# A two-layer hybrid decoder: last down projection and final norm turned from feature-major to token-major

## The chip, the core and the metric

The kernel runs on one core of a Trainium2 chip. The metric is the device time of one execution in microseconds. The core has a matrix engine (TensorE; PE in the rows), a vector engine (VectorE, DVE), an activation engine (ScalarE, ACT), a general engine (GpSimd, POOL), and SyncE (SP), which here only issues DMAs. Each engine works through its own instructions in order; semaphores order the engines among each other. Sixteen DMA engines move data between the device memory and the on-chip memory of 128 partitions. TensorE adds up in PSUM, eight banks of 128 x 512 floats.

## The reference

Input x has 512 tokens and 1024 features, in float32. There are two layers; each has a mixer (three branches, gated and summed) and a feed-forward part, and behind both stands one norm. What the change touches is the end of the second layer:

```python
    x = x + jnp.einsum('bsd,de->bse', merged, w_out[layer])
    h2 = rmsnorm(x, ffn_norm[layer])
    gu = jnp.einsum('bsd,df->bsf', h2, w_gate_up[layer])
    x = x + jnp.einsum('bsf,fd->bsd', jax.nn.silu(gu[..., :D_FF]) * gu[..., D_FF:], w_down[layer])
return rmsnorm(x, final_norm)
```

rmsnorm divides each token's 1024 features by the root of their mean square (plus 1e-6) and multiplies feature by feature with a weight vector. D_FF is 2816, that is 22 tiles of 128.

## The kernel before

Nearly all matmuls are products of split operands. A float32 value is held as a high part (a cast to fp32r) and a low part (the rest), and each product is three matmuls: high by high, high by low, low by high. The weights are split on the chip: `wload` loads 512 KB into `st` (two buffers), ScalarE casts it to `wh`, VectorE subtracts to get `wl` (three buffers each).

**Feature-major.** In most projections (`fm_tile`, `fm_acc`) the stationary operand is a 128x128 piece of a weight tile and the moving operand is an activation tile of 128 features x 512 tokens; a bank then holds 128 output features x 512 tokens. Activations lie in this form too: the residual is eight tiles `xscr[m]` of 128 features x 512 tokens in device memory.

**Token-major.** A few projections of the mixer (`tm_group`) use 128 tokens of the activations as the stationary operand and 512 columns of weights as the moving one, and a bank holds 128 tokens x 512 features.

**The feed-forward part.** A loop over 22 tiles `i` computes a gate tile and an up tile (24 matmuls each, a bank each). VectorE takes the gate out of its bank, ScalarE applies silu, GpSimd multiplies by the norm factor, VectorE multiplies by the up bank; ScalarE and GpSimd split the result into `aH{i}` and `aL{i}`. These intermediate tiles `s` come from a rotating set of five buffers (`rot`). Then the down projection runs over eight output tiles `m`, each 22 x 3 matmuls into one bank. In the second layer the residual tile `xf{m}` is added from its bank, squared on ScalarE, the squares are summed over the tiles by GpSimd and VectorE, and GpSimd multiplies the tile by the final weights. Behind the last tile `Norm.finish` sums over the 128 partitions by matmuls with ones, takes the power -0.5 on GpSimd, and spreads the 512 factors over all partitions by a matmul of ones with diagonal blocks (`dg`). VectorE and GpSimd multiply the eight tiles by the result, and SP stores them. The host transposes the output.

**What sets the order.** TensorE's order is the order in which the `Issue` planner lets the streams issue; in the feed-forward part there is only one stream. On the other engines a scheduler of the framework orders by priority; `wload` asks for high priority, so that loads and casts of weights come early. A load into `st` waits until the buffer's former cast to `wl` is done. Every instruction of the program stands under line 118, that of the helper that records it, so the rows are told apart by tile names.

Of the kernel before, what the change touches and what calls it, by code (L numbers as in the profile page):

```python
# [10 lines left out]
F32 = mybir.dt.float32  # L11
# [25 lines left out]
LAT = 0.7  # L37
DMA_LAT = 2.5
DENSE = 10
PAD = 72  # L40
ORDER = "k z qv0 qv1 aq gv u"


# [5 lines left out]
class Issue:  # L49
# [50 lines left out]
    def bank(self, tag, n, t):  # L100
        self.ready[t.tensor.name] = self.bank_free(tag, n)
        self.banks[tag].append(t.tensor.name)
        return t
# [57 lines left out]

@with_exitstack
def hybrid_kernel(ctx, tc, x0, pos, wi, wkv, wb, wo, wg, wd, gn, convw, lngb, sguw, sgub,
                  sinks, alog, dtb, dnn, out, depth=DEPTH):
    issue = Issue()
    nc = issue.front(tc.nc)
    PSUM = bass.MemoryType.PSUM
# [10 lines left out]
    def nm(s):  # L178
        uid[0] += 1
        return f"{s}_{uid[0]}"  # L180
# [7 lines left out]
    def rot(name):  # L188
        return base.tile([P, T], F32, tag="rot", name=nm(name), bufs=N_ROT)
# [7 lines left out]
    def cst(shape, name, dt=F32):  # L197
        return const.tile(shape, dt, name=name, tag=name)
# [15 lines left out]

    xp = tc.tile_pool(name="x0", bufs=1, reuse_waits="tile")
    x0p = xp.__enter__()
    gnt = cst([P, 2 * DEPTH + 1, KT], "gnt")
    cst([P, PAD], "pad")
    nc.sync.dma_start(gnt, gn)
    xin, kv0 = [], []  # L220
# [133 lines left out]
    def split_hl(k):  # L354
        return (base.tile([P, T], F32R, tag=f"hH{k}", name=nm("hH")),
                base.tile([P, T], F32R, tag=f"hL{k}", name=nm("hL")))

    class Norm:


        def __init__(self, gi, final=False, split=KT - 1):

            self.gi = gi
            self.final = final
            self.split = split
            self.accs = []
            self.xs = []

        def add(self, k, xt):
            g = gnt[:, self.gi, k:k + 1]  # L370
            if not self.final:
                xh, xl = split_hl(k)
                nc.scalar.activation(xh, xt, AF.Copy, scale=g)
                nc.vector.scalar_tensor_tensor(xl, xt, g, xh.bitcast(F32), ALU.mult, ALU.subtract)
                self.xs.append((xh, xl))
            sq = rot("sq")
            nc.scalar.activation(sq, xt, AF.Square)
            if k == 0 or k == self.split < KT - 1:
                self.accs.append(sq)
            else:  # L380
                eng = nc.gpsimd if k < self.split else nc.vector
                eng.tensor_tensor(self.accs[-1], self.accs[-1], sq, ALU.add)
            if k == KT - 1 and len(self.accs) > 1:
                nc.vector.tensor_tensor(self.accs[0], self.accs[0], self.accs[1], ALU.add)
            if self.final:
                nc.gpsimd.tensor_scalar(xt, xt, g, 1.0, ALU.mult, ALU.mult)

        def finish(self):
            ps = bank("px")
# [17 lines left out]
            yield  # L407

    xscr = dram.tile([KT, P, T], F32, name="xscr")


    def layer(l, norm, first=None):
# [715 lines left out]

        nx = Norm(2 * l + 1)
        xold = x0 if l == 0 else xscr  # L1130
        for m in range(KT):
            ps = yield from fm_tile(wo[l, m], ms_)
            xt = rot("xt")
            nc.sync.dma_start(xt, xold[m])
            nc.vector.tensor_tensor(xt, ps, xt, ALU.add)
            nc.sync.dma_start(xscr[m], xt)
            nx.add(m, xt)
        mix.__exit__(None, None, None)


        last = l == depth - 1
        with tc.tile_pool(name=f"ffn{l}", bufs=1, reuse_waits="tile") as fp:
            hx = nx.xs
            issue.spawn(0, nx.finish(), nx.accs[0])
            act = []
            for i in range(KF):
                pgt = yield from fm_tile(wg[l, 2 * i], hx)
                pup = yield from fm_tile(wg[l, 2 * i + 1], hx)
                if i == 0:
                    yield f"rep{nx.gi}"  # L1150
                    rep2 = nx.rep
                s = rot("s")
                nc.vector.tensor_tensor(s, pgt, rep2, ALU.mult)
                nc.scalar.activation(s, s, AF.Silu)
                nc.gpsimd.tensor_tensor(s, s, rep2, ALU.mult)
                nc.vector.tensor_tensor(s, pup, s, ALU.mult)
                ah = fp.tile([P, T], F32R, tag=f"aH{i}", name=nm("aH"))
                al_ = fp.tile([P, T], F32R, tag=f"aL{i}", name=nm("aL"))
                nc.scalar.copy(ah, s)
                nc.gpsimd.tensor_tensor(al_, s, ah.bitcast(F32), ALU.subtract)  # L1160
                act.append((ah, al_))
            nn = Norm(2 * DEPTH if last else 2 * l + 2, final=last)
            xf = []
            for m in range(KT):
                pd = mm_bank()
                for j, (k0, k1) in enumerate(((0, 8), (8, 16), (16, 22))):
                    w = wload(wd[l, m, :, k0 * P:k1 * P], (k1 - k0) * P)
                    yield from fm_acc(pd, w, 0, act[k0:k1], j == 0, j == 2)
                if last:
                    xt = fp.tile([P, T], F32, tag=f"xf{m}", name=nm("xf"))  # L1170
                else:
                    xt = rot("xt")
                nc.sync.dma_start(xt, xscr[m])
                nc.vector.tensor_tensor(xt, pd, xt, ALU.add)
                if not last:
                    nc.sync.dma_start(xscr[m], xt)
                nn.add(m, xt)
                xf.append(xt)
            if last:
                yield from nn.finish()  # L1180
                for m in range(KT):
                    eng = nc.gpsimd if m in (2, 5) else nc.vector
                    eng.tensor_tensor(xf[m], xf[m], nn.rep, ALU.mult)
                    nc.sync.dma_start(out[m], xf[m])
        return nn

    norm = Norm(0, split=4)
    for k in range(KT):
# [14 lines left out]
def _tiles_fm(w):  # L1203

    K, C = w.shape
    return w.reshape(K // P, P, C // P, P).transpose(2, 1, 0, 3).reshape(C // P, P, K)
# [8 lines left out]
def _rep(a):  # L1215
    return np.ascontiguousarray(np.broadcast_to(a[..., None, :], a.shape[:-1] + (P,) + a.shape[-1:]))


def _layout(x, positions, attn_norm, w_in, sgu_ln_g, sgu_ln_b, sgu_w, sgu_b, attn_sinks, dn_conv_w, dn_a_log,
            dn_dt_bias, dn_norm, w_branch, w_out, ffn_norm, w_gate_up, w_down, final_norm):  # L1220
    L = w_in.shape[0]
    cuts = np.cumsum([0, 512, 512, 512, 128, 128, 1536, 512, 4, 4, 3072])
    perm = np.concatenate([np.arange(h * 64, (h + 1) * 64) for h in HEAD_PERM])
    wi, wkv, wb, wg, wd, wo = [], [], [], [], [], []
    for l in range(L):
        u, v, q, k, vb, qkv, z, be, a, gt = [w_in[l][:, cuts[i]:cuts[i + 1]] for i in range(10)]
        wi.append(np.concatenate([_tiles_fm(qkv), _tiles_fm(u), _tiles_tm(q[:, perm]), _tiles_tm(v), _tiles_tm(z),
                                  _tiles_fm(gt)]))
        wkv.append(_tiles_tm(np.concatenate([k, vb, be, a], axis=1)))
        br = []  # L1230
        for i in range(3):
            w = w_branch[l, i][perm] if i == 1 else w_branch[l, i]
            t = _tiles_fm(w)
            br.append(t.reshape(4, 2, P, 512).transpose(0, 2, 1, 3).reshape(4, P, 1024))
        wb.append(np.stack(br))
        wo.append(_tiles_fm(w_out[l]))
        g = _tiles_fm(w_gate_up[l])
        wg.append(np.stack([g[:KF], g[KF:]], axis=1).reshape(2 * KF, P, 1024))
        wd.append(_tiles_fm(w_down[l]))
    gn = np.concatenate([np.stack([attn_norm, ffn_norm], axis=1).reshape(2 * L, D), final_norm[None]])  # L1240
    return {
        "x0": x[0].T.reshape(KT, P, T),
        "pos": positions[0].reshape(NCH, P).T,
        "wi": np.stack(wi), "wkv": np.stack(wkv), "wb": np.stack(wb), "wo": np.stack(wo), "wg": np.stack(wg),
        "wd": np.stack(wd),
        "gn": gn.reshape(2 * L + 1, KT, P).transpose(2, 0, 1),
        "convw": dn_conv_w.reshape(L, 4, 12, P).transpose(0, 3, 2, 1),
        "lngb": np.concatenate([sgu_ln_g, sgu_ln_b], axis=1).reshape(L, 8, P).transpose(0, 2, 1),
        "sguw": sgu_w.transpose(0, 3, 1, 2),
        "sgub": _rep(sgu_b.reshape(L, 512)).reshape(L, P, 4, P),  # L1250
        "sinks": _rep(attn_sinks[:, HEAD_PERM]),
        "alog": _rep(dn_a_log), "dtb": _rep(dn_dt_bias), "dnn": _rep(dn_norm),
    }


_ORDER = ["x0", "pos", "wi", "wkv", "wb", "wo", "wg", "wd", "gn", "convw", "lngb", "sguw", "sgub", "sinks",
          "alog", "dtb", "dnn"]


# [17 lines left out]
```

## Time and profile before

| | |
|---|---|
| time, median of 3 runs | 1768.55 us (1766.57 to 1768.67) |
| profiled execution, own time | 1768.95 us |
| its span | 1767.2 us |
| TensorE busy | 1727.8 us (98%), 8314 matmuls |
| VectorE, ScalarE, GpSimd busy | 876.8 us (50%), 636.9 us (36%), 429.0 us (24%) |
| mean granted TensorE clock | 0.991 |
| DMA | 171.84 MB, mean 97 GB/s; 8000 packets under 512 B |

The span is the time from the first to the last instruction of the profiled execution; its own time is 1.75 us longer. An engine that is busy for half of the span may still set the end in one stretch, so the table is read together with rows by stretch, and with the chain of work that ended last: followed back from the end, at each step to what released it. Ends of matmuls are modelled in this profile, so the pace of matmuls is read from their starts.

### The profile page before, as it was taken

To read this page: it belongs to the slowest core of one execution; us is meant where nothing else is said; L and a number is where in the kernel's file an instruction comes from. 1 tells how busy PE (TensorE), PEld (TensorE's weight loads), DVE (VectorE), ACT (ScalarE), POOL (GpSimd) and SP (SyncE) were. 2 spreads that over 40 slices of the span, in tenths; PEclk is the share of its full clock that TensorE was granted. 3 is DMA by queue.
4 is the path that set the end of the run, shared out by engine and by line. 5 is a ranking of instruction groups with operands and counts; after the bars stand their busy time and mean duration, and the time that the engine had idled before them with its cause. 6 is when DMAs were issued, how large, how long until landed. Compare 5 with 4: busy or idle time off the path is not lost.

```text
span 1767.2 us, 21929 instructions
## 1 busy us (share of the span) xinstructions
PE 1727.8 (98%) x8314; PEld 1427.8 (81%) x8314; DVE 876.8 (50%) x1724; ACT 636.9 (36%) x1171; POOL 429.0 (24%) x463
## 2 busy tenths in 40 slices
PE   8999999999999999999999989999999999999996
PEld 6887778888888888888888877788888888888885
DVE  7695775444543333333277857754445433333222
ACT  5454553322333222222244445632223322222221
POOL 4413321011223333310033133110212233333111
PEclk9999999999999999999999999999999999999998
DMA  4222012223352233334332211122224522333331
GB/s 155 92 98 84 25 37 90 95 89 102 103 178 96 96 97 100 98 115 130 111 114 101 90 52 37 67 84 96 94 97 141 186 95 98 99 102 93 99 94 61
DMA packets 55785, 171.84 MB, mean 97 GB/s; under 512 B 8000, under 2 KB 8256, under 8 KB 55680
## 3 DMA queue, kind: packets, MB, share of 16 engines
q1 hardware_dynamic: 54432, 167.04, 28.9%
q0 software_dynamic: 1248, 3.41, 0.6%
q8 instruction: 65, 1.06, 0.2%
q14 instruction: 40, 0.33, 0.1%
HBM read 159.41 MB, written 11.01 MB: 96 GB/s over the span
## 4 chain that ended last, share of the span: by engine, by line
PE 93%; DVE 4%; ACT 1%; issue 1%; POOL 1%; DMA 0%; SPq 0%; DVEq 0%; POOLq 0%; ACTq 0%
PE mm L118 85%; PE px L118 7%; DVE U L118 1%; DVE wl L118 1%; POOL of L118 0%; DVE pr L118 0%; DVE zg L118 0%; DVE xf L118 0%; DVE Tm L118 0%; ACT pr L118 0%; DMA st<-in_wkv 0%; DVE ys L118 0%; DVE sq L118 0%; DVE S L118 0%; SPq L118 0%
## 5 line engine op out<-in xcount | busy, mean ns | idle before, releaser
L118 ACT CAST wh<-st 128x1024 fp32r<-128x1024 f32 (+2 forms) x288 | 296.2, 1028 | 814.5 <-PE mm L118 731.5
L118 PE MATMUL mm<-hH,wh 128*128 128x512 f32 x1344 | 531.4, 395 | 0.0
L118 PE MATMUL mm<-hH,wl 128*128 128x512 f32 x1344 | 524.0, 390 | 0.0
L118 PE MATMUL mm<-hL,wh 128*128 128x512 f32 x1344 | 523.3, 389 | 0.0
L118 DVE TENSOR_TENSOR wl<-st,wh 128x1024 fp32r<-128x1024 f32 (+2 forms) x288 | 354.5, 1231 | 185.8 <-ACT wh L118 175.7
L118 PEld LDWEIGHTS mm<-hH,wl 128*128 128x128 f32 x1344 | 252.4, 188 | 53.2
L118 PEld LDWEIGHTS mm<-hH,wh 128*128 128x128 f32 x1344 | 252.7, 188 | 52.7 <-issue 2.2
L118 PEld LDWEIGHTS mm<-hL,wh 128*128 128x128 f32 x1344 | 252.8, 188 | 51.8 <-issue 1.5
L118 PE MATMUL mm<-aH,wh 128*128 128x512 f32 x352 | 136.9, 389 | 0.0
L118 PE MATMUL mm<-aL,wh 128*128 128x512 f32 x352 | 136.9, 389 | 0.0
L118 PE MATMUL mm<-aH,wl 128*128 128x512 f32 x352 | 136.9, 389 | 0.0
L118 POOL TENSOR_TENSOR gt<-gt,gt 128x512 f32<-128x512 f32 x32 | 48.8, 1524 | 284.1 <-DVE gt L118 284.1
L118 POOL TENSOR_TENSOR s<-s,rep 128x512 f32<-128x512 f32 x44 | 77.3, 1758 | 162.1 <-ACT s L118 162.1
L118 POOL TENSOR_TENSOR aL<-s,aH 128x512 fp32r<-128x512 f32 x44 | 76.7, 1744 | 156.8 <-ACT aH L118 156.8
L118 PE MATMUL mm<-wh,hH 128*128 128x512 f32 (+1 forms) x256 | 103.1, 403 | 7.1 <-ACT hH L118 7.1
L118 DVE TENSOR_TENSOR s<-mm,s 128x512 f32<-128x512 f32 x44 | 30.4, 692 | 149.2 <-PE mm L118 142.4
L118 DVE TENSOR_TENSOR s<-mm,rep 128x512 f32<-128x512 f32 x44 | 30.4, 692 | 138.2 <-PE mm L118 134.3
L118 POOL TENSOR_TENSOR sq<-sq,sq 128x512 f32<-128x512 f32 x27 | 41.0, 1519 | 235.9 <-ACT sq L118 235.9
L118 PE MATMUL mm<-wh,hL 128*128 128x512 f32 (+1 forms) x256 | 96.7, 378 | 0.2
L118 PE MATMUL mm<-wl,hH 128*128 128x512 f32 (+1 forms) x256 | 96.3, 376 | 0.0
L118 DVE TENSOR_TENSOR gt<-mm,rep 128x512 f32<-128x512 f32 x48 | 33.1, 690 | 107.1 <-PE mm L118 107.1
L118 PEld LDWEIGHTS mm<-aH,wl 128*128 128x128 f32 x352 | 66.1, 188 | 13.8
(256 smaller groups left out, 2325.7 us busy)
## 6 DMA issues: line engine op xcount, KB each, us to landing
st<-in_wi SPq DMA_DIRECT2D x104, 512.0 KB, 3.2
st<-in_wg SPq DMA_DIRECT2D x88, 512.0 KB, 3.2
st<-in_wd SPq DMA_DIRECT2D x32, 512.0 KB, 3.5
st<-in_wb SPq DMA_DIRECT2D x24, 512.0 KB, 3.3
st<-in_wo SPq DMA_DIRECT2D x16, 512.0 KB, 3.3
xscr<-xt SPq DMA_DIRECT2D x24, 256.0 KB, 2.0
st<-in_wd SPq DMA_DIRECT2D x16, 384.0 KB, 3.1
xt<-xscr SPq DMA_DIRECT2D x16, 256.0 KB, 2.8
```

The lines of the kernel that those rows point to most:

```text
L118: return f(*args, **kw)
```

## The change

The second layer's down projection is made token-major. A step of its loop takes one tile of 128 rows of the weights (`wt[k]`, 128x1024) and four blocks of 128 tokens, and adds to eight banks: four blocks by two halves of the 1024 features. The last three weight tiles are held together and used block after block, so that a block is done at a time. Each block's rows are then tokens: the residual is added, ScalarE squares and sums along the row, VectorE multiplies by the final weights (`gft`, the vector repeated on all partitions), GpSimd takes the power of one column, VectorE and ScalarE scale a half each, and SP and ScalarE store a half each. `Norm` loses its final form. The residual must be token-major for this: `residual_tm` is called in the feed-forward loop at i = 4, 6, ..., 18, loads a tile of `xscr`, transposes its 32x32 blocks on VectorE and stores it into `xtok` by four DMAs, each of 32 x 16 runs of 32 floats. `last_down` loads `xtok` in four blocks. `PAD` makes up for the changed sizes of the constants.

```diff
-PAD = 72
+PAD = 48
...
-            if self.final:
-                nc.gpsimd.tensor_scalar(xt, xt, g, 1.0, ALU.mult, ALU.mult)
...
+    xtok = dram.tile([T, D], F32, name="xtok")
...
+                if last and 4 <= i < 4 + 2 * KT and i % 2 == 0:
+                    residual_tm((i - 4) // 2)
+            if last:
+                yield from last_down(fp, act)
+                return None
...
-            if last:
-                yield from nn.finish()
-                for m in range(KT):
-                    eng = nc.gpsimd if m in (2, 5) else nc.vector
-                    eng.tensor_tensor(xf[m], xf[m], nn.rep, ALU.mult)
-                    nc.sync.dma_start(out[m], xf[m])
...
+    def residual_tm(m):
+
+        xt, xb = rot("xt"), rot("xb")
+        nc.sync.dma_start(xt, xscr[m])
+        nc.vector.transpose(xb, xt)
+        for a in range(4):
+            f0 = m * P + 32 * a
+            nc.sync.dma_start(xtok.rearrange("(b i) d -> i b d", i=32)[:, :, f0:f0 + 32],
+                              xb[32 * a:32 * a + 32, :].rearrange("i (b j) -> i b j", j=32))
+
+    def last_down(fp, act):
...
+        gft = fp.tile([P, D], F32, name="gft")
+        nc.sync.dma_start(gft, gf)
+        for c in range(NCH):
+            xt = fp.tile([P, D], F32, tag=f"xf{c}", name=nm("xf"))
+            nc.sync.dma_start(xt, xtok[c * P:(c + 1) * P, :])
+            xs_.append(xt)
+        yield issue.bank_free("mm", 1)
+        banks = [(mm_bank(), bank("px")) for c in range(NCH)]
+
+        def mms(c, k, w):
+            (ah, al_), (wh, wl) = act[k], w
+            tk = slice(c * P, (c + 1) * P)
+            for h in range(2):
+                sl = slice(h * 512, (h + 1) * 512)
+                o = banks[c][h]
+                nc.tensor.matmul(o, lhsT=ah[:, tk], rhs=wh[:, sl], start=k == 0, stop=False)
+                nc.tensor.matmul(o, lhsT=ah[:, tk], rhs=wl[:, sl], start=False, stop=False)
+                nc.tensor.matmul(o, lhsT=al_[:, tk], rhs=wh[:, sl], start=False, stop=k == KF - 1)
+
+        for k in range(KF - 3):
+            w = wload(wt[k])
+            for c in range(NCH):
+                mms(c, k, w)
+                yield
+        ws = [wload(wt[k]) for k in range(KF - 3, KF)]
+        for c in range(NCH):
+            for k in range(KF - 3, KF):
+                mms(c, k, ws[k - KF + 3])
+                yield
+            xt = xs_[c]
+            ss = lay.tile([P, 2], F32, tag="fss", name=nm("fss"), bufs=2)
+            for h in range(2):
+                sl = slice(h * 512, (h + 1) * 512)
+                nc.vector.tensor_tensor(xt[:, sl], banks[c][h], xt[:, sl], ALU.add)
+                sq = rot("sq")
+                nc.scalar.activation(sq, xt[:, sl], AF.Square, accum_out=ss[:, h:h + 1])
+            ms = lay.tile([P, 1], F32, tag="fms", name=nm("fms"), bufs=2)
+            nc.vector.tensor_tensor(ms, ss[:, 0:1], ss[:, 1:2], ALU.add)
+            nc.vector.tensor_scalar(ms, ms, 1.0 / D, EPS, ALU.mult, ALU.add)
+            nc.gpsimd.tensor_tensor(ms, ms, nhalf[:, 0:1], ALU.pow)
+            for h in range(2):
+                sl = slice(h * 512, (h + 1) * 512)
+                nc.vector.tensor_tensor(xt[:, sl], xt[:, sl], gft[:, sl], ALU.mult)
+            nc.vector.tensor_scalar(xt[:, :512], xt[:, :512], ms, None, ALU.mult)
+            nc.sync.dma_start(out[c, :, :512], xt[:, :512])
+            nc.scalar.activation(xt[:, 512:], xt[:, 512:], AF.Copy, scale=ms)
+            nc.scalar.dma_start(out[c, :, 512:], xt[:, 512:])
```

Up to the feed-forward loop of the second layer the order of every engine is the same, but for the loads of `xf` and `gft` on SP. Three places show what moves. The first is SP's queue in that loop, where before there are only loads of gate and up weights (`st`):

```order
L118 DMA st_11892<-in_wg 128x1024
L118 DMA st_11932<-in_wg 128x1024
L118 DMA st_11963<-in_wg 128x1024
L118 DMA st_12003<-in_wg 128x1024
L118 DMA st_12034<-in_wg 128x1024
L118 DMA st_12074<-in_wg 128x1024
```

The same queue after; `xt` is a residual tile, `xb` its transpose:

```order
L118 DMA st_12083<-in_wg 128x1024
L118 DMA xt_12003<-xscr 128x512
L118 DMA st_12114<-in_wg 128x1024
L118 DMA xtok<-xb_12004 32x16x32 x3
L118 DMA st_12162<-in_wg 128x1024
L118 DMA xtok<-xb_12004 32x16x32
L118 DMA st_12193<-in_wg 128x1024
L118 DMA st_12233<-in_wg 128x1024
```

Five DMAs of a panel stand between four weight loads; the stores wait for VectorE's transpose, which waits for the load of `xt`. The second place is SP's queue at the border of the loop and the down projection, before:

```order
L118 DMA st_13170<-in_wg 128x1024
L118 DMA st_13210<-in_wd 128x1024
L118 DMA st_13240<-in_wd 128x1024
L118 DMA st_13270<-in_wd 128x768
L118 DMA st_13301<-in_wd 128x1024
```

and after:

```order
L118 DMA xtok<-xb_13054 32x16x32
L118 DMA st_13235<-in_wg 128x1024
L118 DMA xf_13276<-xtok 128x1024
L118 DMA xf_13278<-xtok 128x1024
L118 DMA xf_13280<-xtok 128x1024
L118 DMA st_13292<-in_wt 128x1024
L118 DMA xf_13282<-xtok 128x1024
L118 DMA st_13322<-in_wt 128x1024
```

The blocks of the turned residual (`xf`) are loaded ahead of the first two weight tiles. The third place is the end of VectorE's queue, before:

```order
L118 TENSOR_TENSOR xf_13937<-mm_13852,xf_13937 128x512
L118 TENSOR_TENSOR sq_13297<-sq_13297,sq_13940 128x512
L118 TENSOR_SCALAR ms_13949<-px_13944 128x4
L118 TENSOR_TENSOR dg_13953<-ident,rst_13951 128x512
L118 TENSOR_TENSOR xf_13294<-xf_13294,rep_13957 128x512
L118 TENSOR_TENSOR xf_13385<-xf_13385,rep_13957 128x512
```

and after, the last of the four blocks and the end of the one ahead of it (`fss` holds the two sums of squares, `fms` the factor):

```order
L118 TENSOR_SCALAR xf_13280<-xf_13280,fms_13975 128x512
L118 TENSOR_TENSOR xf_13282<-mm_13290,xf_13282 128x512
L118 TENSOR_TENSOR xf_13282<-px_13291,xf_13282 128x512
L118 TENSOR_TENSOR xf_13282<-xf_13282,gft 128x512
L118 TENSOR_TENSOR fms_14010<-fss_14003 128x1
L118 TENSOR_TENSOR xf_13282<-xf_13282,gft 128x512
L118 TENSOR_SCALAR fms_14010<-fms_14010 128x1
L118 TENSOR_SCALAR xf_13282<-xf_13282,fms_14010 128x512
```

A block's last instruction on VectorE, the scaling, waits for GpSimd's power of that block, and the next block's first add stands behind it.

## Rows read from the trace of the kernel before

**Rows 1.** The page: shares of the chain that ended last, by engine.

```profile
PE 93%; DVE 4%; ACT 1%; issue 1%; POOL 1%; DMA 0%; SPq 0%; DVEq 0%; POOLq 0%; ACTq 0%
```

**Rows 2.** Stretches: length, busy of PE, PEld, DVE, ACT, POOL; clock, DMA share, GB/s.

```profile
1480.00:1560.00 80.00, 80.00 (x354) 66.25 (x353) 27.96 (x30) 23.95 (x30) 25.26 (x15) 1.00 0.30 99
...
1700.00:1748.00 48.00, 48.00 (x214) 39.74 (x213) 10.93 (x11) 9.60 (x11) 5.88 (x6) 1.00 0.21 60
```

**Rows 3.** Chain of waits behind the last matmul: start, length (us), engine, tile.

```profile
1752.77 1.03 POOL rst L118
...
1754.66 2.06 PE px L118 x2
...
1757.36 0.69 DVE xf L118
```

**Rows 4.** The stores of the output: min/median/max ns of the issue, first and last start.

```profile
L118 SPq DMA_DIRECT2D out<-xf x8: 332/400/464, 1759.2 to 1763.5; - x8
```

**Rows 5.** TensorE in order of time (start, length): mixer's token-major matmuls, then down projection.

```profile
129.07 0.40 PE L118 MATMUL mm<-wl,hH 128*128 128x512 f32 x1
...
130.00 0.40 PE L118 MATMUL mm<-wh,hL 128*128 128x512 f32 x1
...
144.17 0.39 PE L118 MATMUL mm<-wh,hH 128*128 128x512 f32 x1
...
145.75 0.39 PE L118 MATMUL mm<-wl,hH 128*128 128x512 f32 x1
...
1629.18 0.39 PE L118 MATMUL mm<-aH,wh 128*128 128x512 f32 x1
...
1748.63 0.39 PE L118 MATMUL mm<-aH,wl 128*128 128x512 f32 x1
```

**Rows 6.** Groups by shape: count, busy us in all, mean ns of one, idle before.

```profile
L118 DVE TENSOR_SCALAR gv<-gv,mv,rs 128x512 f32<-128x512 f32 x8 | 4.5, 566 | 4.4 <-POOL rs L118 4.4
...
L118 DVE TENSOR_SCALAR rs<-mv 128x1 f32<-128x1 f32 x8 | 1.2, 147 | 0.0
...
L118 DVE STREAM_TRANSPOSE U<-Tm 128x128 f32<-128x128 f32 x32 | 8.3, 288 | 0.1
...
L118 ACT ACTIVATE sq<-xf 128x512 f32<-128x512 f32 x8 | 5.1, 634 | 15.5 <-DVE xf L118 15.5
...
L118 ACT ACTIVATION_READ_ACCUMULATOR ojk<-px 128x1 f32 x64 | 12.5, 195 | 0.0
...
L118 POOL TENSOR_TENSOR rs<-rs,nhalf 128x1 f32<-128x1 f32 x8 | 4.4, 549 | 9.3 <-DVE ng L118 6.1 <-DVE rs L118 2.4 <-DVE rsum L118 0.8
```

**Rows 7.** VectorE, ScalarE and SP in the feed-forward loop, in order of time.

```profile
1603.08 1.22 DVE L118 TENSOR_TENSOR wl<-st,wh 128x1024 fp32r<-128x1024 f32 x1 [0.21 <-ACT wh L118]
1607.69 0.69 DVE L118 TENSOR_TENSOR s<-mm,s 128x512 f32<-128x512 f32 x1 [3.38 <-PE mm L118]
...
1612.87 1.05 ACT L118 CAST wh<-st 128x1024 fp32r<-128x1024 f32 x1 [3.84 <-PE mm L118]
...
1604.33 0.33 SPq L118 DMA_DIRECT2D st<-in_wg  x1
```

**Rows 8.** DMA: two stretches as in rows 2, queue totals, issues (KB, us to landing).

```profile
1759.20:1766.00 6.80, 0.00 (x0) 0.00 (x0) 3.99 (x5) 0.00 (x0) 1.64 (x1) 0.50 0.80 308
...
1440.00:1462.00 22.00, 22.00 (x99) 18.22 (x98) 7.91 (x9) 6.64 (x9) 7.13 (x4) 1.00 0.28 95
...
q1 hardware_dynamic: 54432, 167.04, 28.9%
...
st<-in_wg SPq DMA_DIRECT2D x88, 512.0 KB, 3.2
...
xt<-xscr SPq DMA_DIRECT2D x16, 256.0 KB, 2.8
...
blkscr<-la POOLq DMA_DIRECT2D x16, 128.0 KB, 2.2
...
nx<-blkscr POOLq DMA_DIRECT2D x2, 128.0 KB, 5.1
```

More of the change, by code (lines that the diff above doesn't have):

```diff
@@ L163, in hybrid_kernel @@
 def hybrid_kernel(ctx, tc, x0, pos, wi, wkv, wb, wo, wg, wd, gn, convw, lngb, sguw, sgub,
-                  sinks, alog, dtb, dnn, out, depth=DEPTH):
+                  sinks, alog, dtb, dnn, wt, gf, out, depth=DEPTH):
     issue = Issue()
@@ L216, in hybrid_kernel @@
     x0p = xp.__enter__()
-    gnt = cst([P, 2 * DEPTH + 1, KT], "gnt")
+    gnt = cst([P, 2 * DEPTH, KT], "gnt")
     cst([P, PAD], "pad")
@@ L358, in hybrid_kernel, with __init__ @@
     class Norm:
-        def __init__(self, gi, final=False, split=KT - 1):
+        def __init__(self, gi, split=KT - 1):
             self.gi = gi
-            self.final = final
             self.split = split
@@ L370, in add @@
             g = gnt[:, self.gi, k:k + 1]
[L371 to L375, printed above, removed]
+            xh, xl = split_hl(k)
+            nc.scalar.activation(xh, xt, AF.Copy, scale=g)
+            nc.vector.scalar_tensor_tensor(xl, xt, g, xh.bitcast(F32), ALU.mult, ALU.subtract)
+            self.xs.append((xh, xl))
             sq = rot("sq")
@@ L1130, in layer @@
         xold = x0 if l == 0 else xscr
+        last = l == depth - 1
         for m in range(KT):
@@ L1138, in layer @@
         mix.__exit__(None, None, None)
-        last = l == depth - 1
         with tc.tile_pool(name=f"ffn{l}", bufs=1, reuse_waits="tile") as fp:
@@ L1161, in layer @@
                 act.append((ah, al_))
-            nn = Norm(2 * DEPTH if last else 2 * l + 2, final=last)
-            xf = []
+                if last and 4 <= i < 4 + 2 * KT and i % 2 == 0:
[3 more added lines that the diff above has]
+                return None
+            nn = Norm(2 * l + 2)
             for m in range(KT):
@@ L1168, in layer @@
                     yield from fm_acc(pd, w, 0, act[k0:k1], j == 0, j == 2)
-                if last:
-                    xt = fp.tile([P, T], F32, tag=f"xf{m}", name=nm("xf"))
-                else:
-                    xt = rot("xt")
+                xt = rot("xt")
                 nc.sync.dma_start(xt, xscr[m])
                 nc.vector.tensor_tensor(xt, pd, xt, ALU.add)
-                if not last:
-                    nc.sync.dma_start(xscr[m], xt)
+                nc.sync.dma_start(xscr[m], xt)
@@ L1177, in layer @@
                 nn.add(m, xt)
-                xf.append(xt)
-            if last:
-                yield from nn.finish()
-                for m in range(KT):
-                    eng = nc.gpsimd if m in (2, 5) else nc.vector
-                    eng.tensor_tensor(xf[m], xf[m], nn.rep, ALU.mult)
-                    nc.sync.dma_start(out[m], xf[m])
-        return nn
+        return nn
+    def residual_tm(m):
[6 more added lines that the diff above has]
+                              xb[32 * a:32 * a + 32, :].rearrange("i (b j) -> i b j", j=32))
@@ new lines, in last_down @@
+    def last_down(fp, act):
+        xs_, fin = [], []
+        gft = fp.tile([P, D], F32, name="gft")
[43 more added lines that the diff above has]
+            nc.scalar.dma_start(out[c, :, 512:], xt[:, 512:])
@@ L1238, in _layout @@
         wg.append(np.stack([g[:KF], g[KF:]], axis=1).reshape(2 * KF, P, 1024))
-        wd.append(_tiles_fm(w_down[l]))
-    gn = np.concatenate([np.stack([attn_norm, ffn_norm], axis=1).reshape(2 * L, D), final_norm[None]])
+        if l < L - 1:
+            wd.append(_tiles_fm(w_down[l]))
+    gn = np.stack([attn_norm, ffn_norm], axis=1).reshape(2 * L, D)
     return {
@@ L1245, in _layout @@
         "wd": np.stack(wd),
-        "gn": gn.reshape(2 * L + 1, KT, P).transpose(2, 0, 1),
+        "gn": gn.reshape(2 * L, KT, P).transpose(2, 0, 1),
         "convw": dn_conv_w.reshape(L, 4, 12, P).transpose(0, 3, 2, 1),
@@ L1251, in _layout @@
         "sinks": _rep(attn_sinks[:, HEAD_PERM]),
+        "wt": w_down[L - 1].reshape(KF, P, D), "gf": _rep(final_norm),
         "alog": _rep(dn_a_log), "dtb": _rep(dn_dt_bias), "dnn": _rep(dn_norm),
@@ L1256 @@
 _ORDER = ["x0", "pos", "wi", "wkv", "wb", "wo", "wg", "wd", "gn", "convw", "lngb", "sguw", "sgub", "sinks",
-          "alog", "dtb", "dnn"]
+          "alog", "dtb", "dnn", "wt", "gf"]
 def kernel(**inputs):
@@ L1270 @@
         args.append(nc.dram_tensor(f"in_{name}", a.shape, mybir.dt.from_np(a.dtype), kind="ExternalInput").ap())
-    out = nc.dram_tensor("out", (KT, P, T), F32, kind="ExternalOutput").ap()
+    out = nc.dram_tensor("out", (NCH, P, D), F32, kind="ExternalOutput").ap()
     with tile.TileContext(nc) as tc:
@@ L1275 @@
     o = r.results[0]["out"]
-    return np.ascontiguousarray(o.reshape(D, T).T)[None]
+    return np.ascontiguousarray(o.reshape(T, D))[None]
```

## The prediction

> **What bounds the kernel now.** I read the page first: the chain that ended last is 93% TensorE [rows 1]. Then the busy time by stretches: in the second layer's feed-forward part and in the down projection behind it TensorE is busy for the whole of each stretch at full granted clock, while VectorE is busy for about a third and a fifth, and the DMA engines for 0.30 and 0.21 [rows 2]. So a wait of any other engine there costs nothing until it holds up a matmul. The end is different [rows 3, 4]. The last matmul starts at 1748.63 and ends at about 1749.02 [rows 5]; the span ends at 1767.2. In these 18.2 us there is one chain of small steps: add to the residual, square, sum over features by matmuls with ones, power, diagonal, a 2.06 us product that spreads the factor over the partitions, then eight multiplications and eight stores. The last store is issued at 1763.5, 3.7 us ahead of the end.
>
> **The change, part by part.** *The matmuls.* Before, the projection is 8 tiles of 66 matmuls; after, 22 steps of 24: 528 of 128x512 in both. The feature-major ones have a pitch of (1748.63 - 1629.18) / 527 = 0.2267 us [rows 5]. The trace has token-major ones of the same shape, in the mixers: seven steps in a quiet run take 1.58 us, 0.226 each, and four steps right behind small matmuls 0.93 us, 0.2325 each [rows 5]. The new projection is one quiet run, so I go by the quiet row and add 0.3 us for a change of bank at every third matmul; the other end is 528 x 0.0058 = 3.1 us.
>
> *The feed of the weights* keeps its size: 22 x 512 KB in both. Its play is read in the loop [rows 7]: a load issued at 1604.33 is cast at 1612.87, 8.5 us later, and lands in 3.2 us [rows 8], so it may come 5 us late for nothing. The cast then ends at about 1615.2 and its matmuls start one and a half tiles later, near 1623.7; another 8.5 us. Thirteen or so in all.
>
> *The last three weight tiles* are used block by block, so the third must be cast inside 12 matmuls (2.72 us, 2.95 to the first use of its low part). From TensorE's release to the end of the low part it is 1.05 + 1.22 and three handovers, 2.4 us [rows 7]. It fits with 0.3 to 0.5 us to spare: 0.
>
> *Turning the residual* adds, eight times, one 256 KB load, one VectorE transpose and four stores of 512 runs of 128 B. The nearest row for the transpose is 288 ns for 128x128 [rows 6], so a 128x512 lies between the 0.69 of a plain operation of that size and 4 x 0.288 = 1.15 us; I take 0.75, and it lies in an idle stretch: behind a cast VectorE is idle from 1604.30 to 1607.69 [rows 7]. In the order the load stands behind the weight load that is freed one cast earlier, so it is issued 5 us ahead of its transpose and lands after 2.8 us [rows 8]. Should it be late, VectorE still has 3.4 us before the next eviction, and behind that the evictions of two banks in four. On SP the stores wait for the transpose, and what is queued behind them is a weight load that can't go out until the next cast, 5 us later. Their issue is 0.33 to 0.46 us for 128 runs [rows 4]; if it went with the runs it would be 1.8, four times 7 us in a period of four weight tiles, 21.8 us, and SP does little else. So 0 on the path.
>
> *The packets of these stores* are what the trace does not show. Per panel it is 4 x 512 / 16 = 128 on each DMA engine. A 2 KB packet takes 0.80 x 2048 B x 16 / 308 GB/s = 85 ns of an engine, a 4 KB packet of the weights 0.28 x 4096 x 16 / 95 = 193 ns [rows 8], nearly in proportion, so a 128 B one by itself would be 5 to 10 ns; the mean packet of the queue is 0.289 x 1767.2 x 16 / 54432 = 150 ns. The nearest row is the gather of 2,048 runs of 64 B, 5.1 us to landing where a plain store takes 2.2: 2.9 us for 128 runs on each engine, 23 ns a run [rows 8]. I take 25 to 50 ns, 3 to 6 us per panel; the ends are 0.7 and 19 us. The weights use 0.28 x 21.8 = 6.1 us of the same 21.8. At the value taken the sum is 9 to 12 us of 21.8, and a weight load behind three stores is late by at most 5 us, which is its play: 0.
> The Trainium skill ("DMA: Bandwidth & Descriptors", Specifications) speaks against this part: transfers under 512 B miss the line rate, since the engine reads, modifies and writes. No row of before shows a store of 128 B. If each packet cost twice the 85 ns of the 2 KB one, a panel would fill its period, which is the second rival below; by the gather's row it fills a quarter.
>
> *At the border of the two parts* three loads of the turned residual (1.5 MB) stand on SP between the last feed-forward weights and the first new ones. At 308 GB/s [rows 8] they take 5 us, and the first new weight may only go out one cast (5.4 us) later: 0. The eight loads of 256 KB that stood at the start of the loop go, and were hidden. The banks: the last gate and up banks are evicted within 1 us of their last matmul, and the new projection reaches the fourth of them after 18 matmuls, 4.1 us: 0.
>
> *The tail, removed:* 18.2 us. *Added:* the chain of the last block. With E the end of the last matmul, its first bank is done 0.68 us earlier, and VectorE can start at E - 0.65. Two adds of 0.69 end at E + 0.73. ScalarE's two squares (0.63 each, and 0.19 to read the sum [rows 6]) run beside them and end at E + 1.8; the first weight product ends at E + 1.5. Then the sum of two columns (0.15), the second weight product (0.69), the mean (0.15): E + 2.8. GpSimd's power on one column is 0.55, against 1.03 for four columns [rows 3]: E + 3.45. The scaling, 0.57 on VectorE [rows 6] and some 0.63 on ScalarE, ends at E + 4.1. Then two stores, on two queues. From the last issue to the end it was 3.7 us: E + 7.9. A store issued by ScalarE isn't in this trace; SP's issue is 0.33 to 0.46 us [rows 4], and I take the same, with nothing and twice as much as its ends.
> But VectorE is in order and waits for GpSimd inside a block, so a block holds it from E - 0.65 to E + 4.05, 4.7 us, while TensorE ends one every 18 x 0.2267 = 4.08. The fourth starts 3 x 0.62 = 1.9 us late: E + 9.8. Bounds: no lag, E + 7.9; a scaling, a power and an issue each 0.3 slower in every block, E + 13.
>
> *Sum.* 18.2 - 9.8 = 8.4 us gained, 0.3 lost in the pitch: -8.1. The profiled execution took 1768.95 (span 1767.2 and 1.75 around it), so 1760.9 for its like; the median of the runs is 0.4 lower, so **1760.5 us**.
>
> **The rivals.** *One: token-major matmuls run slower throughout.* For it: every row of them right behind other work is at 0.23; against: the quiet run. At 0.2325 the loss is 3.1 us in place of 0.3: 1763.3.
> *Two, the slow side: the short packets fill the DMA queues.* It decides from (21.8 - 6.1 - 0.7) / 128 = 117 ns per packet. At 150 ns a panel takes 19.2 us, with the weights and the load 26.0 in a period of 21.8: 4.2 us behind, eight times 34, less the 13 of play: TensorE waits 21 us in the loop, 1782. For it: the mean packet of the queue; against: that mean is over packets of 3 KB, and the gather's 23 ns.
> *Three: the turning holds up the feed a little each time*, because load, transpose and stores stand in one line on SP and VectorE. 1 us a panel is 8 us: the gain is eaten, 1768. For it: two in-order queues wait for each other there; against: 13 us of play.
> *Four: the blocks don't lag*, since the scaling or the squares are shorter than their nearest rows: 1758.6.
>
> **How the numbers follow.** The forecast 0.60, rival one 0.13, two 0.07, three 0.08, four 0.12. Differences under 0.2% (3.5 us) can't be told from no change. Faster: the forecast, one and four, 0.85; same: three, 0.08; slower: two, 0.07. The range reaches from under rival four (1757) to a few us above rival one (1766) and leaves out two, three and a little at the lower end.
>
> **What would show it.** In the profile after: TensorE busy without a gap from the feed-forward loop to the last matmul, which ends near 1749.3; transposes of 0.7 to 1.2 us in the gap behind a cast; the 128 B stores landing within 3 to 4 us, with the DMA share in the loop near 0.4 to 0.55; a pitch of 0.227; the last four blocks on VectorE 4.7 us apart and not 4.1; power 0.55; the end 9.8 us behind the last matmul. The forecast is wrong if casts in the loop wait for a DMA and TensorE for casts, or if the last matmul ends later than 1752.

## The result, and the profile after

The changed kernel takes 1757.22 us (median of 4 runs, 1754.46 to 1757.95), the kernel before 1768.61 in the same comparison. The ratio is 0.9933, 95% interval [0.9918, 0.9948]: about 11.9 us or 0.67% faster, where 8.1 us or 0.46% were forecast. Direction and place were right. The size was not, because one step in the tail, the lag of the blocks behind TensorE, did not happen.

The profiled execution took 1757.25 us with a span of 1755.5. Its page, the busy time and the chain by engine (the latter against [rows 1]):

```profile
PE 1724.2 (98%) x8304; PEld 1426.5 (81%) x8304; DVE 881.8 (50%) x1741; ACT 639.6 (36%) x1180; POOL 415.7 (24%) x450
...
PE 93%; DVE 4%; ACT 1%; POOL 1%; issue 1%; DMA 0%; SPq 0%; POOLq 0%; DVEq 0%; ACTq 0%
```

Nothing is to be seen at this level: the shares are those of before. The stretches show the first difference, in the DMA share (columns as in [rows 2, 8]):

```profile
1440.00:1462.00 22.00, 22.00 (x99) 18.23 (x98) 8.53 (x11) 6.41 (x8) 7.38 (x5) 1.00 0.41 120
...
1628.00:1650.00 22.00, 22.00 (x99) 18.23 (x98) 5.59 (x5) 4.76 (x5) 1.79 (x1) 1.00 0.28 96
```

TensorE has the same 99 matmuls in 22 us of the loop as in [rows 8], while the DMA engines are busy for 0.41 in place of 0.28. The first and last matmul of the new projection:

```profile
1628.36 0.39 PE L118 MATMUL mm<-wh,aH 128*128 128x512 f32 x1
...
1747.81 0.39 PE L118 MATMUL px<-wh,aL 128*128 128x512 f32 x1
```

That is 119.45 us for 527 steps, to the hundredth what [rows 5] give for the feature-major projection. From the first matmul of the feed-forward loop to the last of the projection it is 360.67 us in both kernels (1387.14 to 1747.81, and 1387.96 to 1748.63 before). So the whole difference behind the start of the loop lies behind the last matmul. It ends at E = 1747.81 + 0.39 = 1748.20, 7.3 us ahead of the end of the span, where it was 18.2. The four blocks there, VectorE first (start, length, what it waited for), then ScalarE and GpSimd in the last one:

```profile
1735.32 0.69 DVE L118 TENSOR_TENSOR xf<-mm,xf 128x512 f32<-128x512 f32 x1 [1.09 <-PE mm L118]
...
1739.40 0.69 DVE L118 TENSOR_TENSOR xf<-mm,xf 128x512 f32<-128x512 f32 x1
...
1743.48 0.69 DVE L118 TENSOR_TENSOR xf<-mm,xf 128x512 f32<-128x512 f32 x1
...
1747.19 0.49 DVE L118 TENSOR_SCALAR xf<-xf,fms 128x512 f32<-128x512 f32 x1 [0.73 <-POOL fms L118]
1747.60 0.68 DVE L118 TENSOR_TENSOR xf<-mm,xf 128x512 f32<-128x512 f32 x1
1748.23 0.69 DVE L118 TENSOR_TENSOR xf<-px,xf 128x512 f32<-128x512 f32 x1
1749.09 0.69 DVE L118 TENSOR_TENSOR xf<-xf,gft 128x512 f32<-128x512 f32 x1 [0.16 <-ACT sq L118]
1749.71 0.16 DVE L118 TENSOR_TENSOR fms<-fss 128x1 f32<-128x1 f32 x1
1749.79 0.68 DVE L118 TENSOR_TENSOR xf<-xf,gft 128x512 f32<-128x512 f32 x1
1750.39 0.14 DVE L118 TENSOR_SCALAR fms<-fms 128x1 f32<-128x1 f32 x1
1751.27 0.49 DVE L118 TENSOR_SCALAR xf<-xf,fms 128x512 f32<-128x512 f32 x1 [0.73 <-POOL fms L118]
...
1748.33 0.63 ACT L118 ACTIVATE sq<-xf 128x512 f32<-128x512 f32 x1 [0.41 <-DVE xf L118]
1748.87 0.19 ACT L118 ACTIVATION_READ_ACCUMULATOR sq<-xf 128x1 f32 x1
1748.96 0.63 ACT L118 ACTIVATE sq<-xf 128x512 f32<-128x512 f32 x1
1749.50 0.19 ACT L118 ACTIVATION_READ_ACCUMULATOR sq<-xf 128x1 f32 x1
1751.27 0.72 ACT L118 ACTIVATE xf<-xf,fms 128x512 f32<-128x512 f32 x1 [1.58 <-POOL fms L118]
1752.02 0.34 ACTq L118 DMA_DIRECT2D out<-xf  x1
...
1750.68 0.55 POOL L118 TENSOR_TENSOR fms<-fms,nhalf 128x1 f32<-128x1 f32 x1 [3.53 <-DVE fms L118]
```

Look at the starts, not the lengths. On VectorE a large operation of 0.68 us is followed after 0.60 us (1749.79 to 1750.39), a small one of 0.16 after 0.08, the scaling of 0.49 after 0.41. On ScalarE a square of 0.63 is followed after 0.54 and a reading of 0.19 after 0.09. Two starts on VectorE are waits instead: the second add comes 0.03 us behind E, when its bank is done, and the sum of two columns (1749.71) comes 0.02 us behind the end of ScalarE's second reading (1749.50 + 0.19). The blocks begin at 1735.32, 1739.40, 1743.48 and 1747.60: 4.08, 4.08 and 4.12 us apart. TensorE ends a block every 4.08, so the last block is late by 0.05 us, and not by 1.9.

The turning, in the loop (VectorE and SP in order of time; [rows 7] have the same place without it):

```profile
1504.34 1.23 DVE L118 TENSOR_TENSOR wl<-st,wh 128x1024 fp32r<-128x1024 f32 x1 [0.21 <-ACT wh L118]
1505.49 0.70 DVE L118 STREAM_TRANSPOSE xb<-xt 128x512 f32<-128x512 f32 x1
1508.95 0.69 DVE L118 TENSOR_TENSOR s<-mm,s 128x512 f32<-128x512 f32 x1 [2.75 <-PE mm L118]
...
1500.56 0.43 SPq L118 DMA_DIRECT2D xt<-xscr  x1
1505.60 0.33 SPq L118 DMA_DIRECT2D st<-in_wg  x1
1506.22 1.47 SPq L118 DMA_DIRECT2D xtok<-xb  x3
1511.03 0.35 SPq L118 DMA_DIRECT2D st<-in_wg  x1
```

The transpose takes 0.70 us in the idle stretch behind a cast and leaves 2.75 of the 3.4 us; the load was issued 4.9 us earlier; three of the four stores are out 3.3 us ahead of the next weight load, and the fourth follows that load. The 32 stores over the whole kernel:

```profile
L118 SPq DMA_DIRECT2D xtok<-xb x32: 325/478/616, 1440.9 to 1598.5; - x32
...
DMA to landing us min/median/max: 3.1/3.4/5.4
```

### The profile page after: what moved, and what is told of

It is laid out like the page before. It is cut to its first block, busy times and chain, and to the rows that moved or that the text cites. A ratio compares the mean times of both kernels' runs of the same rounds, so it can differ in the third digit from the quotient of the medians.

```text
span 1755.5 us, 21977 instructions
## 1 busy us (share of the span) xinstructions
PE 1724.2 (98%) x8304; PEld 1426.5 (81%) x8304; DVE 881.8 (50%) x1741; ACT 639.6 (36%) x1180; POOL 415.7 (24%) x450
## 4 chain that ended last, share of the span: by engine, by line
PE 93%; DVE 4%; ACT 1%; POOL 1%; issue 1%; DMA 0%; SPq 0%; POOLq 0%; DVEq 0%; ACTq 0%
PE mm L118 83%; PE px L118 11%; DVE U L118 1%; DVE wl L118 0%; POOL of L118 0%; DVE pr L118 0%; DVE zg L118 0%; DVE Tm L118 0%; ACT wh L118 0%; ACT pr L118 0%; DVE xf L118 0%; DMA st<-in_wkv 0%; DVE ys L118 0%; DVE S L118 0%; DVE sq L118 0%
## 5 line engine op out<-in xcount | busy, mean ns | idle before, releaser
L118 PE MATMUL mm<-brH,wh 128*128 128x512 f32 x192 | 74.7, 389 | 0.0
L118 PE MATMUL mm<-brL,wh 128*128 128x512 f32 x192 | 74.7, 389 | 0.0
L118 PE MATMUL mm<-brH,wl 128*128 128x512 f32 x192 | 74.7, 389 | 0.0
L118 POOL TENSOR_TENSOR sq<-sq,sq 128x512 f32<-128x512 f32 x21 | 33.3, 1585 | 156.4 <-ACT sq L118 156.4
L118 PE MATMUL mm<-aH,wh 128*128 128x512 f32 x176 | 68.5, 389 | 0.0
```

The lines of the kernel that those rows point to most:

```text
L118: return f(*args, **kw)
```

## The experiments

### Is the turning free, and is the tail all of the gain?

**The changed kernel again, twice** (no edit).

> The changed kernel once more, unchanged, beside the kernel before. In the profiles the span is 11.7 us shorter: 10.9 us of it lie behind the last matmul, 0.8 us ahead of the first changed instruction. If the tail is all that the change gives, the ratio over more runs is about 1 - 10.9 / 1768.6 = 0.9938. If the earlier part gains too, it is 0.9933 or lower.

> The changed kernel unchanged, beside the kernel of this call and the kernel before: ratio to before 0.9938 if the tail is all of the gain; the kernel of this call 0.7 us (0.04%) faster than this one, not to be told by the clock.

Measured: 0.9931 [0.9918, 0.9944], 1756.48 us, and 0.9934 [0.9922, 0.9947], 1757.02 us. From the end of the last matmul to the end of the span it is 7.3 and 7.4 us again. The 0.9938 of the tail alone lies inside all three intervals, but every estimate is a little under it. In the profiles of these three the feed-forward loop starts at 1387.14, 1386.36 and 1386.07; in the two with the old projection at 1387.96 and 1387.78; in the variants below between 1386.57 and 1389.57. That is a scatter of 3.5 us ahead of nearly every changed instruction. Over all nine profiles with the new projection the mean of that start is 1387.7, over the two with the old one 1387.9, so the profiles show no gain ahead of the loop beyond their scatter. So 10.9 us are shown, and about 1 us is left open: scatter, or a little in the part before.

**The kernel before with the turning only:**

```diff
...
                 act.append((ah, al_))
+                if last and 4 <= i < 4 + 2 * KT and i % 2 == 0:
+                    residual_tm((i - 4) // 2)
...
```

> The kernel before with the turning of the residual added (eight loads, transposes and 32 stores in the feed-forward loop) and its result not used; projection and norm as before. Theory 'the turning is free': as before, ratio 0.999 to 1.001 (1768.6 us), no gap of TensorE in the loop, the stores land in 3 to 4 us. Rival 'the turning costs a little and the new tail gains more than it seems': ratio over 1.002 (1772 us or more).

Measured: 1768.08 us, ratio 0.9995 [0.9986, 1.0004]. By the interval the turning costs at most 0.04%, 0.7 us. The loop of this kernel:

```profile
1440.00:1462.00 22.00, 22.00 (x99) 18.23 (x98) 8.52 (x10) 6.62 (x9) 7.13 (x4) 1.00 0.41 119
```

The same DMA share as in the changed kernel and the same full TensorE; from the loop's start to the last matmul 360.67 us. The stores land in 3.4 us (median).

**The changed kernel without the turning:**

```diff
-                if last and 4 <= i < 4 + 2 * KT and i % 2 == 0:
-                    residual_tm((i - 4) // 2)
...
-            nc.sync.dma_start(xt, xtok[c * P:(c + 1) * P, :])
+            nc.sync.dma_start(xt, xscr.rearrange("k (p two) t -> (k p) (two t)", two=2)[c * P:(c + 1) * P, :])
```

> The changed kernel without the turning: the four blocks are loaded from the residual as it lies in memory, in wrong order, so the output is not the reference's. Theory 'the turning is free': as the changed kernel, 1757.2 us within 2. Rival 'the turning costs': shorter by what it costs, 1753 us or less.

Measured: 1758.0 us, 0.9938 [0.9924, 0.9952]; loop and projection 360.66 us. Nothing comes back when the turning goes, so it costs nothing on this side either.

### What do the blocks of the tail cost?

**The last weight tiles not held for one block:**

```diff
-        for c in range(NCH):
-            for k in range(KF - 3, KF):
+        for k in range(KF - 3, KF):
+            for c in range(NCH):
                 mms(c, k, ws[k - KF + 3])
                 yield
+        for c in range(NCH):
             xt = xs_[c]
```

> The changed kernel, but the last three weight tiles are gone through for all four blocks one after the other, as the first nineteen are, so that the blocks are complete 6 matmuls (1.36 us) apart and not 18 (4.08 us). Theory 'VectorE's time per block is the sum of starts, about 3.1 us, where it need not wait': the order now lays the next block's adds into the wait for GpSimd, so from E - 4.7 four blocks take 12.4 us and the end is 11 to 12 us behind the last matmul (7.3 in the changed kernel), 1761.5 us. Rival 'a block holds VectorE for its whole chain, 4.1 us, whatever the order': 15 us behind the last matmul, 1765 us. Rival 'blocks one behind the other are worth nothing, TensorE sets the pace': 7.3 to 8.5 us, 1757 to 1758.

Measured: 1763.04 us, ratio 0.9970 [0.9959, 0.9981]; the end is 13.5 us behind the last matmul (1750.27 to 1763.8). It met none of the three. VectorE from the first add to the last scaling:

```profile
1745.55 0.69 DVE L118 TENSOR_TENSOR xf<-mm,xf 128x512 f32<-128x512 f32 x1 [9.25 <-PE mm L118]
...
1750.97 0.16 DVE L118 TENSOR_TENSOR fms<-fss 128x1 f32<-128x1 f32 x1 [0.28 <-ACT sq L118]
...
1759.51 0.48 DVE L118 TENSOR_SCALAR xf<-xf,fms 128x512 f32<-128x512 f32 x1 [0.73 <-POOL fms L118]
```

Four blocks take 14.4 us, 3.6 each: less than the chain's 4.1, since the next block's adds now fill the wait for the power, and more than the 3.1 of bare starts, since the squares stand behind the last block's scaling on ScalarE and VectorE waits for them (0.28 us, three times), and the last block's power has nothing to fill it. What follows is a split of the gain: 4.7 us (18.2 to 13.5) come with the token-major form of projection and norm, even with the blocks ending 1.36 us apart (VectorE begins 4.7 us ahead of the end of the last matmul), and 6.2 us (13.5 to 7.3) come from holding the last three weight tiles, so that blocks end 4.08 us apart and three of the four are done under the matmuls.

**Two more operations in each block:**

```diff
+                nc.vector.tensor_tensor(xt[:, sl], xt[:, sl], gft[:, sl], ALU.mult)
                 nc.vector.tensor_tensor(xt[:, sl], xt[:, sl], gft[:, sl], ALU.mult)
```

> The changed kernel with each block's two products by the final weights done twice on VectorE (the output carries the weights squared). In the changed kernel a block's instructions on VectorE take 4.07 us from first to first and TensorE ends a block every 4.08, so the two are level. Theory 'an operation costs the time from its start to the next start (0.61 us), not its duration (0.69), and what does not fit into the wait for GpSimd pushes the next block': blocks 4.5 to 4.7 us apart, the last scaling 2.0 us later, the end 9.3 us behind the last matmul (7.3 in the changed kernel). Theory of the prediction, durations added: 2.8 us later, 10.1 behind. Rival 'TensorE sets the pace and VectorE has room': blocks still 4.1 apart, 7.7 behind.

Measured in one execution: the last matmul ends at 1749.55, the span at 1759.9, 10.35 us later. The first add of each block and the scalings of the second, third and last on VectorE, then one of GpSimd's powers:

```profile
1736.67 0.69 DVE L118 TENSOR_TENSOR xf<-mm,xf 128x512 f32<-128x512 f32 x1 [1.09 <-PE mm L118]
...
1741.74 0.69 DVE L118 TENSOR_TENSOR xf<-mm,xf 128x512 f32<-128x512 f32 x1
...
1746.57 0.49 DVE L118 TENSOR_SCALAR xf<-xf,fms 128x512 f32<-128x512 f32 x1 [0.45 <-POOL fms L118]
1746.97 0.68 DVE L118 TENSOR_TENSOR xf<-mm,xf 128x512 f32<-128x512 f32 x1
...
1751.02 0.48 DVE L118 TENSOR_SCALAR xf<-xf,fms 128x512 f32<-128x512 f32 x1
1751.42 0.68 DVE L118 TENSOR_TENSOR xf<-mm,xf 128x512 f32<-128x512 f32 x1
...
1755.63 0.48 DVE L118 TENSOR_SCALAR xf<-xf,fms 128x512 f32<-128x512 f32 x1
...
1745.53 1.00 POOL L118 TENSOR_TENSOR fms<-fms,nhalf 128x1 f32<-128x1 f32 x1 [4.82 <-DVE fms L118]
```

The blocks are 5.07, 5.23 and 4.45 us apart: TensorE doesn't set the pace, and a lag like the one that the prediction described appears as soon as a block needs more than 4.08 us. But my new number fell too: the end moved by 3.0 us, not 2.0, near the 2.8 of the sum of durations. Where nothing is waited for, the starts are 0.60 to 0.61 us apart as the theory has it; what it left out is that the power, with a product on VectorE beside it, takes 0.86 to 1.00 us in place of 0.55. In each of the first two blocks the scheduler laid one product beside the power, and VectorE waits 0.45 us for it; in the last two it laid two products there, and VectorE doesn't wait. So the order is not the same in all four blocks, the longer power accounts for most of the missing 1.0 us, and the sum of durations came close for a wrong reason.

**One small operation fewer:**

```diff
-                nc.scalar.activation(sq, xt[:, sl], AF.Square, accum_out=ss[:, h:h + 1])
+                nc.scalar.activation(sq, xt[:, sl], AF.Square, scale=D ** -0.5, accum_out=ss[:, h:h + 1])
...
-            nc.vector.tensor_tensor(ms, ss[:, 0:1], ss[:, 1:2], ALU.add)
-            nc.vector.tensor_scalar(ms, ms, 1.0 / D, EPS, ALU.mult, ALU.add)
+            nc.vector.scalar_tensor_tensor(ms, ss[:, 0:1], EPS, ss[:, 1:2], ALU.add, ALU.add)
```

> The changed kernel with one small operation fewer in each block: the squares are scaled so that their sums are the means, and one instruction adds both and the epsilon. So the power no longer waits for the second product by the weights, which stands ahead of the second small instruction. Theory 'the chain behind the last matmul runs through that product': the power starts 0.7 us earlier, the blocks need 3.4 us of VectorE and wait for TensorE, the end is 6.6 us behind the last matmul (7.3), 0.04% of the time, not to be told by the clock. Rival 'VectorE and GpSimd share their way to memory, so the power waits for the product beside it': the power takes 0.9 us or more and the end stays at 7.2 or later.

Measured: 1756.35 us, 0.9927 [0.9914, 0.9939]. The last block:

```profile
1749.14 0.16 DVE L118 SCALAR_TENSOR_TENSOR fms<-fss 128x1 f32<-128x1 f32 x1
1749.22 0.68 DVE L118 TENSOR_TENSOR xf<-xf,gft 128x512 f32<-128x512 f32 x1
1750.34 0.49 DVE L118 TENSOR_SCALAR xf<-xf,fms 128x512 f32<-128x512 f32 x1 [0.44 <-POOL fms L118]
...
1749.38 0.93 POOL L118 TENSOR_TENSOR fms<-fms,nhalf 128x1 f32<-128x1 f32 x1 [3.15 <-DVE fms L118]
```

E is 1747.62. The power starts at E + 1.76, 0.72 earlier than in the changed kernel, as expected, but takes 0.93 us beside the product. The scaling starts at E + 2.72 (E + 3.07 before) and the end is at E + 7.0: both theories hold a part.

**The halves one after the other:**

```diff
-            for k in range(KF - 3, KF):
-                mms(c, k, ws[k - KF + 3])
-                yield
+            for h in range(2):
+                for k in range(KF - 3, KF):
+                    mms(c, k, ws[k - KF + 3], (h,))
+                    yield
...
```

> As the one before, and in the last three weight tiles a block's first half is finished (9 matmuls) before its second, so that add, square and product of the first half lie 2 us ahead of the block's end. Theory 'behind the last matmul only add, square, power and scaling of the second half count': add ends at E + 0.7, square at E + 1.4, scaling starts at E + 2.3, the end is 6.2 to 6.6 us behind the last matmul. Rival 'the first half was in the way': 0.5 us or more earlier than the kernel without it.

Measured: 1758.04 us, 0.9940 [0.9926, 0.9953]; the end is at E + 7.0, the scaling at E + 2.72, both as in the kernel without this edit, so the first half was not in the way. That it is no faster has another cause: loop and projection now take 361.78 us, 1.1 more.

```profile
1732.83 0.44 PE L118 MATMUL mm<-wh,aH 128*128 128x512 f32 x1
1734.04 0.50 PE L118 MATMUL mm<-wl,aH 128*128 128x512 f32 x1 [0.77 <-DVE wl L118]
```

TensorE waits for the last weight tile's low part, which is now wanted 6 matmuls (1.36 us) earlier. At a pitch of 0.23 us the matmul would have started at 1733.06, so it is 0.98 us late, and the margin of the changed kernel's order is 1.36 - 0.98, about 0.4 us. The changed kernel's own rows say the same; there the low part ends at 1734.23 and is first used at 1734.66:

```profile
1733.00 1.23 DVE L118 TENSOR_TENSOR wl<-st,wh 128x1024 fp32r<-128x1024 f32 x1 [4.21 <-ACT wh L118]
...
1734.66 0.39 PE L118 MATMUL mm<-wl,aH 128*128 128x512 f32 x1
```

The prediction had 0.3 to 0.5.

**The second half's weights behind the power:**

```diff
-            for h in range(2):
-                sl = slice(h * 512, (h + 1) * 512)
-                nc.vector.tensor_tensor(xt[:, sl], xt[:, sl], gft[:, sl], ALU.mult)
-            nc.vector.tensor_scalar(xt[:, :512], xt[:, :512], ms, None, ALU.mult)
+            nc.vector.tensor_tensor(xt[:, :512], xt[:, :512], gft[:, :512], ALU.mult)
+            nc.vector.scalar_tensor_tensor(xt[:, 512:], xt[:, 512:], ms, gft[:, 512:], ALU.mult, ALU.mult)
...
```

> On top of the kernel with one small operation: the second half is no longer multiplied by the final weights ahead of the power; VectorE multiplies it by factor and weights in one instruction behind the power, and ScalarE scales the first half. Nothing then runs on VectorE beside the power. Theory 'the power took 0.93 us and not 0.55 because VectorE worked beside it': the power is 0.55 again, the scaling starts at E + 2.35 (E + 2.72 with the product beside it, E + 3.07 in the changed kernel), the end is 6.6 us behind the last matmul. Rival 'the power is slow for the sum that ScalarE or VectorE has just written': still 0.93, the end at 7.0 or later, since the one instruction is 0.2 us longer than the scaling.

Measured: 1756.9 us, 0.9929 [0.9916, 0.9943], E = 1749.66. The last power, the last instruction on VectorE, and the stores:

```profile
1751.42 0.55 POOL L118 TENSOR_TENSOR fms<-fms,nhalf 128x1 f32<-128x1 f32 x1 [3.53 <-DVE fms L118]
...
1752.00 0.75 DVE L118 SCALAR_TENSOR_TENSOR xf<-xf,fms,gft 128x512 f32<-128x512 f32 x1 [0.66 <-POOL fms L118]
...
L118 ACTq DMA_DIRECT2D out<-xf x4: 362/368/402, 1740.5 to 1752.8; - x4
L118 SPq DMA_DIRECT2D out<-xf x4: 332/338/345, 1740.6 to 1752.8; - x4
...
DMA to landing us min/median/max: 2.5/2.7/2.8
```

The power is 0.55 us again and the scaling starts at E + 2.34: the theory holds, and it is VectorE's product beside it that slows it. Yet the end is at E + 7.0, not 6.6. Both halves are now ready at the same moment, their stores are issued together and land in 2.5 to 2.8 us, where the changed kernel, with 0.25 us between them, had 2.0 to 2.4. What was won ahead of the stores was mostly lost in them. This kernel and the one with one small operation fewer have a tail shorter by 0.3 us than the changed kernel in the profile; against a scatter of some us from run to run the times can't show that.

## Why the prediction was right and wrong

*The matmuls: right, a shade high.* 0.3 us were put on the pitch; it is 0.2267 to the last digit, and rival one is out.

*The feed, the border and the last three weight tiles: right.* TensorE waits for nothing from the loop's start to the last matmul; the margin at the last tiles is 0.4 us, inside the 0.3 to 0.5 that were read.

*The turning: right.* 0 on the path, by both halves of the test. The packets, which no row showed, cost (0.41 - 0.28) x 22 = 2.9 us of the engines per panel, 0.7 of it for the load, so 2.2 us for 128 packets on each engine: 17 ns a packet, under the 25 to 50 taken and far from the 117 from which rival two would decide. The store is slow per byte: 128 B in 17 ns on 16 engines is 120 GB/s, against 385 by the same reckoning for the 2 KB in 85 ns.
The Trainium skill's rule ("DMA: Bandwidth & Descriptors", Specifications) that runs under 512 B miss the line rate agrees with these 120 GB/s; it does not say what the path loses, and here that was nothing. One reading of the prediction was off: by the gather's 23 ns a panel's stores take 2.9 us of 21.8, an eighth of the period and not a quarter.

*The tail: the step that failed.* "a block holds it from E - 0.65 to E + 4.05, 4.7 us, while TensorE ends one every 18 x 0.2267 = 4.08. The fourth starts 3 x 0.62 = 1.9 us late: E + 9.8." Measured E + 7.3. The 2.5 us divide so: the lag was 0.05 in place of 1.9; the chain of one block ended 0.4 earlier (last issue at E + 3.8 with no lag, forecast E + 4.2); the way from the last issue to the end was 3.5, not 3.7. The lag and the chain have one root. I added durations; on ScalarE and on VectorE the next operation starts before the last one's duration is over. In the last block, from its first add: the sum of two columns starts after 2.11 us (2.48 reckoned), the mean after 2.79 (3.32), the power after 3.08 (3.55), the scaling after 3.67 (4.14), and the next block's add would come after 4.08 (4.70). Up to the sum the chain runs through ScalarE's two squares, and 0.37 us are saved there; VectorE saves 0.16 from the sum to the mean and 0.15 behind the scaling; the power comes 0.06 later behind the mean than reckoned. An error of 0.62 us in one block was multiplied by three, because the block sat just at the pace of TensorE: what is a little over lags three times, what is level lags not at all. The experiment with two more operations shows that a lag comes back once a block is longer than 4.08. Rival four, no lag, at 1758.6, is what happened; its reason (shorter scaling or squares) was only a part of it: the scaling gave 0.15 of the 0.62, and the squares are not shorter (0.63 and 0.19, as in [rows 6]) but follow each other sooner.

*The rest.* Of 11.9 us by the ratio the tail explains 10.9. The range began at 1757; the ratio of 0.9933, taken on the 1768.55 from which the prediction started, is 1756.7. A tail that was off by 2.5 us together with the open 1 us used the range up: it was cut close on the side to which the sum of durations could only err.

## What to carry to other kernels

Take the time of a chain on one engine from the starts of successive operations in the trace, not from their durations. Where work is handed on in blocks, compare the consumer's time per block with the producer's first: when they are level, a small error decides between no lag and a lag that grows with every block, so the range must hold both. And before calling a tail a sum, ask which of its parts run beside each other: here the power beside a product, and two stores beside each other, took longer than apart.

## What the runs showed of the hardware

- GpSimd's power on one column takes 0.55 us alone and 0.86 to 1.00 us while VectorE multiplies 128x512 floats in the on-chip memory.
- Back to back, VectorE's 128x512 operations of 0.68 us start 0.60 to 0.61 us apart, and a one-column operation of 0.16 us is followed after 0.08. ScalarE's square of 0.63 us is followed after 0.54, its reading of the sum (0.19) after 0.09.
- Two stores of 256 KB issued together on two queues land in 2.5 to 2.8 us, with 0.25 us between them in 2.0 to 2.4.
- Stores in runs of 128 B cost the DMA engines about 17 ns a run, beside a stream of weights at 95 GB/s.
